# State space stage of a hybrid diffusion block: context chunks transposed first, last product of a group in the large accumulators

## The chip, the core and the metric

The kernel runs on one core of a Trainium2 chip. The metric is the device time of one execution in microseconds. TensorE (PE) does matrix products and transposes into PSUM accumulators, VectorE (DVE) and ScalarE (ACT) do elementwise work and empty the accumulators, GpSimd (POOL) does masks and small sums, and SyncE (SP) issues nearly all DMAs. Each engine takes its instructions in the order in which they were written for it.

## What is computed

One layer of a diffusion backbone over 512 latent tokens and 256 context tokens of width 1024, in fp32 throughout. The part that matters here is the bidirectional state space scan (SSD) in the token mixer, with 24 heads in 4 groups and chunks of 128 tokens. In the reference, for one direction:

```
cb = jnp.einsum('bctgn,bcsgn->bctsg', cc, bc)
y_diag = jnp.einsum('bctsg,bctsgh,bcsghp->bctghp', cb, decay, xdt)
states = jnp.einsum('bcsgn,bcsgh,bcsghp->bcghpn', bc, decay_end, xdt)
...
h_final, h_prev = lax.scan(step, h0, (jnp.moveaxis(chunk_decay, 1, 0), jnp.moveaxis(states, 1, 0)))
y_off = jnp.einsum('bctgn,bctgh,bcghpn->bctghp', cc, jnp.exp(acum), h_prev)
y = (y_diag + y_off).reshape(bn, length, nh, hp)
```

The scan over the latent tokens starts from the final states of the context's two chunks. Ahead of the scan lie one wide input projection and a short convolution with silu; behind it a gate `silu(z)`, two branch projections and a mix, and then 16 routed experts (two matrices up, one down).

## The kernel before

The program runs in stages: modulation and the first projections (to about 90 us), the SSD stage (to about 380 us), gates and the Fourier branch, the branch projections and the mix (to about 620 us), routing, and the experts.

In the SSD stage `ssd(g)` works on one group of heads, g = 0 to 3, and is woven with the *fill*: the z tiles of the group before (`zgate`, 3 tiles z00, z01, z02 for group 0) and the input projections of the next group (`xbc_tiles`, 5 tiles pj and the context's pjc). The weave alternates the two in the order of the program; the scheduler then places each engine's instructions by priority and readiness, and that order is fixed when the kernel is built. A fill tile is 24 products of 128x512 in three passes (lines 348, 349, 350), with its weights split into a high and a low part by ACT and DVE (lines 276, 277, tile whl).

A group goes through these steps:
- *Transposes* (line 542): six chunks, four of the sequence (c = 0 to 3) and two of the context (c = 4, 5). Four transposes fill one accumulator ptr, which ACT copies out (line 544) to xb, or for the context to the spare ends of Hf and Hb.
- *Context states* pcs (line 559): the context chunks weighted by DVE (xwc, line 550) and multiplied; then the *states* pst (line 566) of the sequence's chunks, chunk by chunk in both directions, each with DVE's weighting and two DVE steps for the decay (568, 571).
- *Masks* rm: for each chunk and each half of the heads a DMA brings rows of decays (line 588) into one of four slots, POOL masks them (589, 591), DVE and ACT add and exponentiate (593, 595, 597), and DVE multiplies (598, 599, 602). A mask is named by group, chunk and half: rm020 is group 0, chunk 2, first half.
- *Products* py (line 612): for each chunk 36 small products into one accumulator, half of them with each of the chunk's masks, which DVE then adds into the result (line 615). py03 is chunk 3 of group 0.

PSUM has eight accumulators of 512 columns in two pools, each handed out in turn: five `mm`, called large here (`MM`), for the projections and other wide products, and three `sd` (`SD`), for everything in `ssd`. With three, an accumulator asked for now is the one that was asked for three requests ago. A product py needs 384 of 512 columns.

Of the kernel before, what the change touches and what calls it, by code (L numbers as in the profile page):

```python
# [26 lines left out]
NCH = 4  # L27
# [34 lines left out]
def block_kernel(ctx: ExitStack, tc: tile.TileContext, a: dict, out: bass.AP):  # L62
# [18 lines left out]
    def SD(name):  # L81
        return ps.tile([P, 512], F32, name=name, tag="sd")
# [4 lines left out]
    def v(t, off, *dims):  # L87

        n = int(np.prod(dims))
        s = t[:, off:off + n]  # L90
        if len(dims) == 2:
            return s.rearrange("p (a b) -> p a b", b=dims[1])
        if len(dims) == 3:
            return s.rearrange("p (a b c) -> p a b c", b=dims[1], c=dims[2])
        return s
# [435 lines left out]
    def ssd(g):  # L531
# [2 lines left out]
        xb = S(f"xb{g}", 4)  # L534
        Hs = [S(f"Hf{g}", 5), S(f"Hb{g}", 6)]
        with tc.high_priority():
            for c in range(6):
                p = SD(f"ptr{g}_{c}")
                for i in range(4):
                    src = X[:, 512 * i + 128 * c:512 * i + 128 * c + 128] if c < 4 else \  # L540
                        B[g][:, 512 + 256 * i + 128 * (c - 4):512 + 256 * i + 128 * (c - 3)]
                    pe.transpose(p[:, 128 * i:128 * i + 128], src, ident)
                dst = xb[:, 512 * c:512 * c + 512] if c < 4 else Hs[c - 4][:, 1536:2048]
                act.copy(dst, p)
# [16 lines left out]
        for k in range(3):  # L561
            for d in range(2):
                c, n = (k, k + 1) if d == 0 else (3 - k, 2 - k)
# [39 lines left out]
                yield mk[:, 0], rb  # L603

        def products(c, parts):
            py = SD(f"py{g}{c}")
            for b, (mk, rb) in enumerate(parts):
                for hb in range(3):
                    h = 3 * b + hb
                    i, j = divmod(h, 2)  # L610
                    for k, (l, r) in enumerate(((tok(c), mk), (H(0, c), rb[:, 0]), (H(1, c), rb[:, 1]))):
                        pe.matmul(py[64 * j:64 * j + 64, 128 * i:128 * i + 128], lhsT=l[:, 64 * h:64 * h + 64], rhs=r[:, hb],  # L612
                                  start=(k == 0), stop=(k == 2))
            yv = X[:, 0:1536].rearrange("p (i t) -> p i t", i=3)[:, :, 128 * c:128 * c + 128]
            dve.tensor_add(yv, yv, v(py, 0, 3, 128))
# [4 lines left out]
        for c in range(NCH):  # L620
            nxt = list(decays(c + 1)) if c + 1 < NCH else None
            yield
            products(c, parts)
            parts = nxt
            yield
# [70 lines left out]
    for g in range(G):  # L696
        weave(PAT[g], ssd(g), chained(*([zgate(g - 1, 8 * g - 3)] if g else []), *([xbc_tiles(g + 1)] if g + 1 < G else [fourier_in()])))
# [279 lines left out]
    def softmax(c):  # L977
        def negmax_exp():
            dve.tensor_reduce(st[:, c, 0:1], aff[c], axis=AX.X, op=ALU.max, negate=True)
            act.activation(aff[c], aff[c], AF.Exp, bias=st[:, c, 0:1], accum_out=st[:, c, 1:2])  # L980
        return (lambda: dve.scalar_tensor_tensor(aff[c], lg[c][:, 128:128 + NE], rsd[:, c + 1, 1:2], lb, op0=ALU.mult,
                                                 op1=ALU.add),
                negmax_exp,
                lambda: dve.reciprocal(st[:, c, 1:2], st[:, c, 1:2]),
                lambda: dve.tensor_scalar_mul(aff[c], aff[c], st[:, c, 1:2]))
# [42 lines left out]
    f = softmax(0)  # L1028
# [474 lines left out]
```

## Time and profile before

| | |
|---|---|
| median of 3 runs | 1098.39 us (1098.13 to 1099.03) |
| the profiled execution | 1095.86 us, of which the span from first to last instruction is 1094.1 |
| PE busy | 1064.9 us, 97% of the span |
| DVE, ACT, POOL busy | 520.0, 431.5, 86.0 us |
| DMA | 293.82 MB, 269 GB/s over the span |

The busy time of PE is modelled: its matmuls overlap, so that one of 128x512 lasts 0.39 us but the next starts 0.23 us later. A wait of PE stands in square brackets behind the instruction that waited, with the instruction that released it.

### The profile page before, as it was taken

The numbers are of one execution on the slowest core, as the hardware profiler recorded it, in microseconds if no ns is written. First come the engines' busy times: TensorE is split into PE (matmuls) and PEld (weight loads), VectorE is DVE, ScalarE is ACT, GpSimd is POOL, SyncE is SP. The second block draws the span as 40 slices with busy tenths as digits, with TensorE's granted clock in tenths as the row PEclk, the third lists the DMA queues.
The fourth block names the chain that finished last, engine by engine and source line by source line (L and its number), as shares of the span: only waits on it lengthen the run. The fifth ranks groups of instructions, "written<-read, shape, count | busy, mean of one in ns | idle before, by whom it ended". The sixth has DMA issues, their size and how long they took to land.

```text
span 1094.1 us, 15349 instructions
## 1 busy us (share of the span) xinstructions
PE 1064.9 (97%) x6154; PEld 712.4 (65%) x6154; DVE 520.0 (48%) x853; ACT 431.5 (39%) x690; POOL 86.0 (8%) x119
## 2 busy tenths in 40 slices
PE   8999999999999999999999999999999999899997
PEld 5788867878878888888788634454545454444444
DVE  5776989786695666864434531212121212120206
ACT  4467786795794543242323631212021211021112
POOL 1001143021112100000100200000000000000000
PEclk9999999999999999999999999999999999999999
DMA  9613251422514358863337899999999999999996
GB/s 358 232 39 99 72 143 49 115 88 88 171 45 134 126 219 297 314 238 116 98 113 293 324 402 422 407 422 420 421 421 420 422 421 421 420 421 421 421 415 273
DMA packets 57590, 293.82 MB, mean 269 GB/s; under 512 B 6992, under 2 KB 15664, under 8 KB 30256
## 3 DMA queue, kind: packets, MB, share of 16 engines
q1 hardware_dynamic: 56800, 290.65, 68.6%
q10 hardware_dynamic: 720, 2.21, 0.6%
q8 instruction: 48, 0.79, 0.3%
q14 instruction: 22, 0.18, 0.1%
HBM read 288.52 MB, written 4.31 MB: 268 GB/s over the span
## 4 chain that ended last, share of the span: by engine, by line
PE 49%; issue 43%; DVE 3%; DMA 3%; ACT 1%; POOL 1%; POOLq 0%; SPq 0%; ACTq 0%
PE gt L350 3%; PE gt L348 3%; PE gt L349 3%; PE py L612 2%; PE pj L348 2%; PE pj L349 2%; PE pj L350 2%; DMA rm<-rowd 2%; PE sbr L350 2%; PE sbr L349 2%; PE sbr L348 2%; PE z L348 2%; PE z L350 2%; PE z L349 2%; PE pst L566 2%
## 5 line engine op out<-in xcount | busy, mean ns | idle before, releaser
L1338 DVE TENSOR_TENSOR hid<-hid,pu 128x512 f32<-128x512 f32 x16 | 11.0, 687 | 231.5 <-PE pu L1166 231.5
L1377 PE MATMUL pd<-w_ed,hidT 128*64 128x256 f32 x1024 | 115.8, 381 | 4.9 <-DMA w_ed<-in_w_ed_dram 4.7
L276 ACT CAST whl<-raw 128x1024 fp32r<-128x1024 f32 x71 | 74.4, 1050 | 114.3 <-PE gt L350 46.7
L1166 PE MATMUL pu<-w_eu,xes 128*64 128x512 f32 x512 | 115.3, 595 | 3.5 <-DMA w_eu<-in_w_eu_dram 3.5
L277 DVE TENSOR_TENSOR whl<-raw,whl 128x1024 fp32r<-128x1024 f32 x71 | 90.5, 1277 | 48.1 <-ACT whl L276 47.9
L1166 PE MATMUL pg<-w_eg,xes 128*64 128x512 f32 x512 | 111.9, 594 | 0.0
L1377 PEld LDWEIGHTS pd<-w_ed,hidT 128*64 128x64 f32 x1024 | 73.5, 137 | 43.9 <-DMA w_ed<-in_w_ed_dram 7.6
L1166 PEld LDWEIGHTS pu<-w_eu,xes 128*64 128x64 f32 x512 | 36.9, 137 | 75.8 <-issue 66.7
L1166 PEld LDWEIGHTS pg<-w_eg,xes 128*64 128x64 f32 x512 | 36.0, 137 | 69.7 <-issue 65.8
L1298 DVE SCALAR_TENSOR_TENSOR ys<-pd,afs,ys 128x512 fp32r<-128x512 f32 (+1 forms) x18 | 12.4, 691 | 111.4 <-ACT ys L1297 111.4
L1348 ACT COPY hidT<-ht 128x512 f32<-128x512 f32 x16 | 9.4, 586 | 125.5 <-PE ht L1346 125.5
L1297 ACT ACTIVATE ys<-pd,afs 128x512 fp32r<-128x512 f32 (+1 forms) x18 | 11.5, 640 | 102.7 <-PE pd L1377 61.4
L350 PE MATMUL gt<-hhi,whl 128*128 128x512 f32 x128 | 50.0, 391 | 0.0
L348 PE MATMUL gt<-hhi,whl 128*128 128x512 f32 x128 | 50.0, 391 | 0.0
L593 DVE TENSOR_TENSOR rm<-rm,misc 128x768 f32<-128x768 f32 x32 | 32.4, 1014 | 36.8 <-POOL rm L591 36.8
L349 PE MATMUL gt<-hlo,whl 128*128 128x512 f32 x128 | 49.8, 389 | 0.0
L348 PE MATMUL pj<-hhi,whl 128*128 128x512 f32 x120 | 48.6, 405 | 0.0
L350 PE MATMUL pj<-hhi,whl 128*128 128x512 f32 x120 | 48.2, 402 | 0.0
L349 PE MATMUL pj<-hlo,whl 128*128 128x512 f32 x120 | 48.0, 400 | 0.0
L671 DVE SCALAR_TENSOR_TENSOR wm<-wm,misc 128x1024 f32<-128x1024 f32 x32 | 38.1, 1221 | 13.4 <-DMA wm<-in_wmod_dram 13.4
L1320 ACT ACTIVATE hid<-pg 128x512 f32<-128x512 f32 x16 | 9.4, 597 | 82.4 <-PE pg L1166 82.4
L348 PE MATMUL z<-hhi,whl 128*128 128x512 f32 x96 | 41.3, 430 | 0.0
(436 smaller groups left out, 2301.1 us busy)
## 6 DMA issues: line engine op xcount, KB each, us to landing
w_eg<-in_w_eg_dram SPq DMA_DIRECT2D x64, 1024.0 KB, 19.8
w_eu<-in_w_eu_dram SPq DMA_DIRECT2D x64, 1024.0 KB, 19.8
w_ed<-in_w_ed_dram SPq DMA_DIRECT2D x56, 1024.0 KB, 19.8
raw<-in_w_rest_dram SPq DMA_DIRECT2D x71, 512.0 KB, 3.3
wm<-in_wmod_dram SPq DMA_DIRECT2D x16, 1024.0 KB, 6.8
rm<-rowd SPq DMA_DIRECT2D x32, 384.0 KB, 5.3
wmod<-in_wmod_dram SPq DMA_DIRECT2D x8, 1024.0 KB, 7.9
w_ed<-in_w_ed_dram SPq DMA_DIRECT2D x16, 512.0 KB, 10.9
```

The costliest lines, as they stand in the source:

```text
L276: act.copy(hi, src)
L277: dve.tensor_sub(lo, src, hi.bitcast(F32))
L348: pe.matmul(dst, lhsT=wh, rhs=hi, start=(kt == 0 and start), stop=False)
L349: pe.matmul(dst, lhsT=wh, rhs=lo, start=False, stop=False)
L350: pe.matmul(dst, lhsT=wl, rhs=hi, start=False, stop=(kt == nk - 1 and stop))
L566: pe.matmul(p[:, 0:384], lhsT=tok(c)[:, 384:512], rhs=t, start=True, stop=True)
L593: dve.tensor_tensor(mk, mk, csm[:, :, c, hs:hs + 3][:, :, :, None].to_broadcast([P, 2, 3, 128]), op=ALU.add)
L612: pe.matmul(py[64 * j:64 * j + 64, 128 * i:128 * i + 128], lhsT=l[:, 64 * h:64 * h + 64], rhs=r[:, hb], start=(k == 0), stop=(k == 2))
L671: dve.scalar_tensor_tensor(wv, wv, 1.0, crow, op0=ALU.mult, op1=ALU.mult, accum_out=mod2[:, 2 * p + s:2 * p + s + 1])
L1166: pe.matmul(pout[n][64 * e:64 * e + 64, :], lhsT=xe[kt // 4][:, kt % 4, 64 * e:64 * e + 64], rhs=w[kt // 2, e][:, o:o + 512], start=(kt == ...
L1298: dve.scalar_tensor_tensor(R(yl_), pd, afs, yh_, op0=ALU.mult, op1=ALU.subtract)
L1377: pe.matmul(pd[64 * e:64 * e + 64, o:o + 256], lhsT=hidT[kt // 4][:, kt % 4, 64 * e:64 * e + 64], rhs=wd[m, e][:, 256 * kt:256 * kt + 256] ...
```

## The change

Two lines of `ssd`. The context's chunks are transposed ahead of the sequence's, and the accumulator of the last product of each group (chunk 3) is asked for in the large pool.

```
-            for c in range(6):
+            for c in (4, 5, 0, 1, 2, 3):
                 p = SD(f"ptr{g}_{c}")
...
         def products(c, parts):
-            py = SD(f"py{g}{c}")
+            py = (MM if c == NCH - 1 else SD)(f"py{g}{c}")
```

No instruction is added or left out, but the scheduler places many of them anew. The first place is PE between groups 0 and 1, from the last products of py01 on. A row names the accumulator, then the two operands; z00 is the first fill tile of group 1's weave, ptr1_4 and ptr1_5 are the context chunks of group 1. Before:

```order
L612 MATMUL py01_1281<-rm011_1063,xb0_794 64x128
L612 MATMUL py01_1281<-rm011_1063,Hf0_795 64x128
L612 MATMUL py01_1281<-rm011_1063,Hb0_796 64x128
L348 MATMUL z00_1470<-hhi0_205,whl5_1472 128x512
L349 MATMUL z00_1470<-hlo0_207,whl5_1472 128x512
L350 MATMUL z00_1470<-hhi0_205,whl5_1472 128x512
L348 MATMUL z00_1470<-hhi0_205,whl5_1472 128x512
```

And in the changed kernel:

```order
L612 MATMUL py01_1281<-rm011_1063,xb0_794 64x128
L612 MATMUL py01_1281<-rm011_1063,Hf0_795 64x128
L612 MATMUL py01_1281<-rm011_1063,Hb0_796 64x128
L612 MATMUL py02_1329<-rm020_1220,xb0_794 64x128
L542 MATMUL ptr1_4_1372<-mats_92,B1_896 128x128 x4
L542 MATMUL ptr1_5_1378<-mats_92,B1_896 128x128 x4
L612 MATMUL py02_1329<-rm020_1220,Hf0_795 64x128
```

The 24 products of z00 and the first 3 of z01, which stood between py01 and py02, now stand behind: the first three of z00 come after the first half of py03, and when the state products pst of group 1 begin 12 z products have run where 60 had run before. On ACT the copies of these transposes stand behind the exponential (line 597) of the first mask of group 1, in the changed kernel:

```order
L597 ACTIVATE rm100_1505<-rm100_1505 128x768
L544 COPY Hf1_1370<-ptr1_4_1372 128x512
L544 COPY Hb1_1371<-ptr1_5_1378 128x512
L544 COPY xb1_1369<-ptr1_0_1384 128x512
L544 COPY xb1_1369<-ptr1_1_1390 128x512
```

Before, the same exponential stood ahead of them too, with the copies of ptr1_0 and ptr1_1 as the first. On DVE, at the masks of chunks 2 and 3 of group 0 (whl7 is the weight of z02):

```order
 L598 TENSOR_TENSOR rm021_1234<-rm021_1234 128x384
-L277 TENSOR_TENSOR whl7_1598<-raw_899,whl7_1598 128x1024
+L598 TENSOR_TENSOR rm030_1301<-rm030_1301 128x384
 L599 TENSOR_TENSOR rm021_1234<-rm021_1234,cb0_890 128x384
-L598 TENSOR_TENSOR rm030_1301<-rm030_1301 128x384
+L599 TENSOR_TENSOR rm030_1301<-rm030_1301,cb0_890 128x384
 L602 TENSOR_TENSOR rm030_1301<-rm030_1301,B0_656 128x768
```

A weight split leaves its place between the two halves of a mask and moves behind group 1's first states. Up to this place, from the first products of group 0 on, DVE's instructions are the same in number and nearly the same in order. Between groups 1 and 2, and 2 and 3, the last projection tile (pj24, pj34) stands behind the last product (py13, py23) in both kernels; now two transposes of each context chunk stand right behind the first product of py12 (py22), and the chunks of the sequence other than the first close up behind 18 products of pj24 (pj34). From the z tiles of group 3 on the order is the same in both kernels.

## Rows read from the trace of the kernel before

**Rows 1.** The page: span, and busy us of each engine (share)

```profile
span 1094.1 us, 15349 instructions
PE 1064.9 (97%) x6154; PEld 712.4 (65%) x6154; DVE 520.0 (48%) x853; ACT 431.5 (39%) x690; POOL 86.0 (8%) x119
```

**Rows 2.** Windows: us, busy us (instructions) by engine, PEclk, DMA share, GB/s

```profile
99.50:142.90 43.40, 42.80 (x255) 33.85 (x253) 41.50 (x66) 37.35 (x49) 10.50 (x15) 1.00 0.42 121
137.00:164.00 27.00, 24.69 (x159) 18.29 (x158) 24.20 (x33) 23.45 (x32) 11.10 (x13) 1.00 0.53 144
547.00:600.00 53.00, 52.94 (x234) 43.48 (x233) 20.55 (x22) 15.97 (x23) 5.16 (x4) 1.00 0.53 195
700.00:800.00 100.00, 99.66 (x606) 48.30 (x603) 15.44 (x23) 13.95 (x30) 0.00 (x0) 1.00 1.01 417
```

**Rows 3.** Waits of SP's queue on the experts' weights: us, times, longest

```profile
SPq L1158 <- PE mix L823: 16.9, 1, 16.9
```

**Rows 4.** PE timeline (start, us): its waits in the SSD stage from 100 us on

```profile
143.11 0.40 PE L612 MATMUL py<-rm,xb 128*64 128x128 f32 x2 [0.57 <-DVE rm L599]
...
156.68 0.33 PE L542 MATMUL ptr<-mats,B 128*128 128x128 f32 x1 [0.28 <-DVE A L615]
...
160.39 0.59 PE L559 MATMUL pcs<-xwc,Hf 128*128 128x384 f32 x1 [0.77 <-DVE xwc L550]
...
163.25 0.59 PE L559 MATMUL pcs<-xwc,Hf 128*128 128x384 f32 x1 [0.69 <-DVE xwc L550]
...
221.25 0.33 PE L542 MATMUL ptr<-mats,A 128*128 128x128 f32 x1 [0.75 <-DVE A L615]
...
299.42 0.33 PE L542 MATMUL ptr<-mats,A 128*128 128x128 f32 x1 [0.80 <-DVE A L615]
...
359.50 0.29 PE L612 MATMUL py<-rm,xb 128*64 128x128 f32 x1 [0.70 <-DVE rm L599]
```

**Rows 5.** PE timeline between groups 0 and 1

```profile
136.12 0.50 PE L348 MATMUL z<-hhi,whl 128*128 128x512 f32 x1
...
142.15 0.39 PE L350 MATMUL z<-hhi,whl 128*128 128x512 f32 x1
...
144.53 0.50 PE L348 MATMUL z<-hhi,whl 128*128 128x512 f32 x1
...
150.68 0.66 PE L542 MATMUL ptr<-mats,A 128*128 128x128 f32 x4
```

**Rows 6.** Windows of the z tiles' instructions alone

```profile
136.12:143.11 6.99, 6.42 (x27) 4.99 (x27) 0.00 (x0) 1.00 0.67 186
```

**Rows 7.** DVE timeline: first context weighting of group 0, masks of chunk 2

```profile
100.19 0.56 DVE L550 TENSOR_TENSOR xwc<-Hf,misc 128x384 f32<-128x384 f32 x1 [0.82 <-ACT Hf L544]
...
142.42 0.55 DVE L599 TENSOR_TENSOR rm<-rm,cb 128x384 f32<-128x384 f32 x1
...
145.89 1.21 DVE L277 TENSOR_TENSOR whl<-raw,whl 128x1024 fp32r<-128x1024 f32 x1
147.02 0.55 DVE L599 TENSOR_TENSOR rm<-rm,cb 128x384 f32<-128x384 f32 x1
```

**Rows 8.** ACT timeline: exponential of rm100, and the first copy behind it

```profile
152.06 0.84 ACT L597 ACTIVATE rm<-rm 128x768 f32<-128x768 f32 x1 [0.74 <-POOL rm L591]
154.01 0.59 ACT L544 COPY xb<-ptr 128x512 f32<-128x512 f32 x1 [1.10 <-PE py L612]
```

**Rows 9.** SP timeline: the load of mask rm100

```profile
144.75 0.36 SPq L588 DMA_DIRECT2D rm<-rowd  x1
```

**Rows 10.** Windows: the clock behind the mix

```profile
620.00:632.00 12.00, 10.09 (x77) 5.21 (x70) 9.06 (x34) 8.95 (x27) 2.39 (x5) 0.86 1.00 417
```

**Rows 11.** PE timeline: the longest wait in that stretch

```profile
627.26 0.29 PE L989 MATMUL lg<-mats,affs 128*48 128x128 f32 x1 [0.94 <-DVE affs L985]
```

## The prediction

> **What bounds the kernel now.** I read the page's busy table first: PE is busy 97% of a span of 1094.1 us [rows 1], so time is lost only where PE waits or works slower, and what another engine does counts only through a PE wait. Then the windows: around the SSD stage PE and DVE are both near full. From 99.5 to 142.9 us DVE is busy 41.50 of 43.40 us, and from 137 to 164 PE loses 2.3 of 27 us [rows 2]. Later, from 700 us on, the 16 DMA engines are at 1.01 with PE at 99.66 of 100 us [rows 2], which asks whether a shift of the SSD stage reaches the end at all. It does: the loads of that stretch go out when PE's mixing products free their buffers (the sync queue waited 16.9 us for one) [rows 3], and in between, at 547 to 600 us, PE has next to no slack (52.94 of 53 us) while DMA stands at 0.53 [rows 2]. So a microsecond that PE wins or loses in the SSD stage is a microsecond at the end, less nothing that I can point to.
>
> Last the PE timeline of the SSD stage: it shows seven waits, 4.56 us together [rows 4]. Three of them (0.28, 0.75, 0.80) are a transpose that waits for DVE's add of line 615, that is for the small accumulator that the last product of the group ahead still holds; two (0.77, 0.69) are the context state products behind their DVE weighting; two (0.57, 0.70) are a chunk product behind the mask on DVE. The change can win back 1.83 us of the first kind and 1.46 of the second, and by luck 0.57 more ahead of them: the whole prize is 0.3%.
>
> **What is removed and added.** No instruction is removed or added: the same transposes, copies, products and adds, an accumulator of the same size in another pool. What changes is the order, and the printed order tells most. I go by boundary between groups.
>
> Boundary 0 to 1, the first two excerpts. In the kernel before, product py01 ends as the z tiles begin, at 136.12 [rows 5]; PE then runs 27 matmuls of z00 and z01 (6.42 us busy in 6.99) [rows 6] and only then, at 143.11, the first product of py02, which even so waits 0.57 us [rows 4]: its mask rm020 is multiplied on DVE from 142.42 to 142.97 [rows 7]. In the changed kernel py02 stands right behind py01, and no z matmul comes before half of py03. My reading is that py03 now asks for a buffer of the large pool ahead of z00 in program order, and z00 can no longer overtake it; but whatever made it, the order is fixed and PE takes its matmuls as they stand. So the question is when rm020 is ready. On DVE it is row 192 in both orders, with the same work ahead of it, and DVE has only 1.90 us of idle time in 99.5 to 142.9 that it could have saved [rows 2]; 0.82 us of that is the start, where the first weighting waits for the copy of a context chunk [rows 7], which the change brings ahead. Against it, the bias of tile pj11 on ACT now stands behind more copies, and DVE's next instruction wants it. I take 0.5 us earlier.
> - First wait: 143.11 less 136.12 is 6.99, less 0.5 gives **6.5 us** in which PE has nothing (bounds 5.1, if DVE saves all 1.90, and 7.5, if the copies make it 0.5 later).
> - Second wait: py02's second half needs rm021, ready at 147.57 [rows 7]. The 1.21 us weight split between moves away and a 0.55 us add comes in, so 146.9. PE starts at 142.6 and has half a product (143.11 to 144.53, 1.42 us [rows 4, 5]) and two transposed context chunks (0.66 us busy for one such, a little less back to back [rows 5]), so it is there at 145.3. **1.6 us** (0.5 to 2.2).
> - Third wait: ptr1_1 needs the bank of ptr1_4, whose copy on ACT stands behind the exponential of rm100 (the excerpt on ACT). That one was at 152.06, after a mask whose load went out at 144.75 [rows 8, 9], just behind py02's first half. That half now ends 0.7 us later, so the exponential of 0.84 ends at 153.6 and a copy of 0.59 [rows 8] at 154.1; PE, from 146.9, has two half products and one more with a transposed chunk in it (3 x 1.42 and 0.66), and 8 z matmuls at 0.232 (26 of them from 136.12 to 142.15 [rows 5]), so it arrives at 153.7. **0.4 us** (0 to 1.1).
> - Removed here: 0.57, 0.28, 0.77 and 0.69, together **2.3 us**. The context transposes come long before their weighting now, and the split that stood ahead of it on DVE is gone.
> - Net at this boundary: 6.5 + 1.6 + 0.4 - 2.3 = **+6.2 us**. The 48 z matmuls that are left over cost nothing extra (PE must run them in any case), but they do not win it back either: behind this place the kernel before has only 2.25 us of waits left in the stage [rows 4].
>
> Boundaries 1 to 2 and 2 to 3. Here the tile pj24 (pj34) stood behind py13 (py23) already, so no filler is lost. The transposes of context chunks begin in front of py12's body, in banks that are long free, and the waits of 0.75 and 0.80 [rows 4] for line 615 go, since the bank of py13 is not theirs any more. In exchange ptr2_1 stands three short matmuls behind the last piece of ptr2_4 and must wait for its 0.59 us copy [rows 8]: 0.2 us each. **-1.15 us** for both (bounds -1.55 and 0). The wait of 0.70 at 359.50 hangs on the mask alone and stays.
>
> The clock. The granted clock is 1.00 through the whole stage now [rows 2]. It is 0.86 in 620 to 632 us, where PE waits 0.94 us for DVE among small products [rows 10, 11]; 12 us at 0.86 is at most 1.7 us of PE work lost. An idle stretch of 6.5 us is far longer than any that PE has in the stage. I expect 1.2 GHz for a while behind it, part of it inside the second wait: **+0.5 us** (0 to 1.7).
>
> Sum: 6.2 - 1.15 + 0.5 = **+5.5 us**. The profiled execution took 1095.86 us for its span of 1094.1, so 1101.4 by it; the median of the runs shown is 1098.39, 2.5 us above that execution, so I forecast **1103.9 us**, 0.5% slower. With all low ends: 5.1 + 0.5 - 2.3 - 1.55 = +1.75, 1100.1 us. With all high ends: 7.5 + 2.2 + 1.1 - 2.3 + 1.7 = +10.2, 1108.6 us.
>
> **The rivals.** Less than 0.2%, 2.2 us, is about what a measurement of this kernel can tell from no change.
>
> The prize alone, faster: the masks of chunk 2 are ready when py01 ends, because ACT and DVE run their share of group 0 earlier. Then the waits of transposes and weightings go (2.3 + 1.15) and nothing is added: 1098.39 - 3.45 = 1094.9 us. It decides from the point where rm020 is ready by 136.2, 6.8 us earlier than now; DVE's 1.90 us of idle time [rows 2] speak against it. For it speaks only that the profile's times are of one order of instructions, and this is another. 5%.
>
> Low ends together, about the same: ACT's copies do come early, DVE closes all its gaps, no second halt of note, and both later boundaries win their full share: +1.75, 1100.1 us. 15%.
>
> A long cold stretch: if the clock falls not once but again, since the second and third waits follow closely, two more pieces such as that of 620 to 632 cost 2 x 1.7 us less the 0.7 that the waits hide: +8.2, 1106.6 us. For it: between 136 and 154 PE would have 8.5 us of waits and then mostly small products, which is what stands around 627 too [rows 10]. Against it: no drop in the stage now, with waits up to 0.8. 25%. The Trainium skill, page "TensorE: Matmul & The Clock Gate", section "HAM oscillation — how this bites in real kernels", describes it as a habit: matmuls that wait long for data fall back to half rate at every such wait and restart cold. By that rule this rival would be the likelier, and the forecast 1106.6 rather than 1103.9; the drop near 627 agrees in kind, but no row here has a wait as long as this one.
>
> The change does little at the later boundaries (the transposes wait for ACT's copies in place of DVE's adds): that puts 1.15 us on any of these cases, and is inside their spread.
>
> **How the numbers follow.** My own sum 55%, the cold stretch 25%, the low ends 15%, the prize alone 5%. The forecast is the first, with 1101 to 1106 us as its own range. The range of 8 in 10 leaves out the prize (5%), the lowest part of the low ends and the highest of the cold stretch: 1099.8 to 1107.5 us. Slower by over 0.2% (above 1100.6 us) are the first two cases: 80%, and 0.03 of the low ends, about 82%; same 13%; faster 5%.
>
> **What would show it.** After: a PE wait of 5 to 7.5 us near 136 us, put down to DVE's line 599 and standing ahead of a py product; a second of 1 to 2 us some 3 us behind it; no wait on line 615 for a transpose near 221 and 300; z matmuls from about 150 us on instead of 136; a granted clock under 1.00 just behind the first wait. The state products of group 1 then start earlier than now (165.12) by some 5 us but with 48 z matmuls (11.1 us at 0.232) still to come. I am wrong if PE reaches py02 later than I think, if masks come several microseconds earlier, or if PE's delay is absorbed behind 600 us, where loads and PE run level.

## The result, and the profile after

The changed kernel takes 1106.95 us (median of 4 runs, 1104.88 to 1108.5) against 1098.71 us for the kernel before in the same comparison: 1.0072 times as long, 95% interval 1.0056 to 1.0088. That is 8.2 us slower, where 5.5 were forecast. The profiled execution of the changed kernel is the slowest of its four (1108.5 us) and that of before was a quick one (1095.86 us), so the two profiles lie further apart than the medians.

The page of the changed kernel, as [rows 1]:

```profile
span 1106.8 us, 15368 instructions
PE 1067.4 (96%) x6151; PEld 714.3 (65%) x6154; DVE 516.4 (47%) x853; ACT 428.9 (39%) x688; POOL 92.8 (8%) x119
```

PE's busy time is 2.5 us above that of before, while the span has grown by 12.7. Most of what was lost is PE standing still. Where, the PE timeline of the SSD stage tells (start, duration, and in brackets the idle time ahead and what ended it), as [rows 4]:

```profile
142.94 0.66 PE L612 MATMUL py<-rm,xb 128*64 128x128 f32 x2 [6.51 <-DVE rm L599]
...
155.32 0.92 PE L542 MATMUL ptr<-mats,A 128*128 128x128 f32 x6 [0.89 <-ACT Hf L544]
...
160.30 0.88 PE L559 MATMUL pcs<-xwc,Hf 128*128 128x384 f32 x2 [1.50 <-DVE xwc L550]
...
235.39 0.89 PE L559 MATMUL pcs<-xwc,Hf 128*128 128x384 f32 x2 [1.68 <-DVE xwc L550]
...
237.61 1.65 PE L559 MATMUL pcs<-xwc,Hb 128*128 128x384 f32 x2 [1.34 <-DVE xwc L550]
...
314.00 0.44 PE L542 MATMUL ptr<-mats,B 128*128 128x128 f32 x2 [0.73 <-ACT B L362]
...
319.15 0.91 PE L559 MATMUL pcs<-xwc,Hb 128*128 128x384 f32 x2 [1.21 <-DVE xwc L550]
```

Seven waits again, but now 13.9 us together instead of 4.6. The three on DVE's line 615 are gone, and so is the 0.70 at 359.50. In their place stand one of 6.51 ahead of py02, two ahead of group 1 (a transpose that waits for ACT's copy, and a context product pcs), and waits at the context products of groups 2 and 3 and at a transpose of group 3.

The windows, as [rows 2] for the first two; the other two are the stretches in which the clock was low:

```profile
99.50:142.90 43.40, 36.93 (x226) 28.95 (x224) 41.07 (x66) 37.32 (x49) 11.52 (x15) 0.98 0.44 121
137.00:164.00 27.00, 18.67 (x122) 13.76 (x123) 23.07 (x35) 18.85 (x29) 9.41 (x12) 0.87 0.39 107
141.20:148.00 6.80, 5.06 (x34) 4.43 (x35) 6.80 (x11) 5.87 (x8) 2.45 (x3) 0.50 0.22 84
236.75:243.60 6.85, 5.99 (x11) 3.79 (x12) 5.67 (x10) 2.17 (x4) 0.00 (x0) 0.50 0.23 74
```

From 137 to 164 PE is busy 18.67 of 27 us where it was 24.69. The granted clock is 0.50, that is 1.2 GHz, for 6.8 us around the end of the first wait, and for 6.85 us again from 236.75 on, at the pair of waits of 1.68 and 1.34.

The shift can be followed along PE by the starts of products that both kernels have. This table is read from the PE timelines of all runs (us; fa is the first product of the Fourier branch behind the stage; in g0_small_mask_late the first transposes of the stage already start 1.5 us later than in before, at 96.90 against 95.40):

| run | py11 | py21 | py31 | end of py33 | fa |
|---|---|---|---|---|---|
| before | 192.4 | 270.5 | 342.9 | 362.1 | 384.3 |
| after | 200.3 | 283.3 | 356.1 | 374.0 | 396.2 |
| after_again | 200.2 | 279.2 | 352.1 | 370.0 | 392.2 |
| order_only | 193.1 | 270.9 | 343.4 | 361.4 | 383.6 |
| pool_only | 200.0 | 278.1 | 352.9 | 370.8 | 393.0 |
| g0_small | 192.1 | 271.2 | 343.7 | 361.6 | 383.8 |
| g0_only | 200.0 | 278.2 | 350.7 | 369.2 | 391.4 |
| warm_wait | 200.2 | 278.6 | 352.1 | 370.0 | 392.2 |
| z00_ahead | 196.4 | 275.1 | 347.8 | 366.7 | 388.9 |
| z00_z01_ahead | 192.9 | 271.9 | 346.3 | 364.3 | 386.4 |
| after_mask_late | 199.6 | 277.4 | 349.1 | 367.1 | 389.3 |
| order_mask_late | 193.0 | 270.4 | 341.9 | 359.8 | 382.0 |
| g0_small_mask_late | 195.2 | 272.4 | 344.0 | 361.9 | 384.1 |
| z00_z01_ahead_mask_late | 192.6 | 270.3 | 341.9 | 360.0 | 382.2 |

In the first two rows: 7.9 us are lost by py11, another 4.9 between py11 and py21, 0.5 by py31, and 1.3 come back by the end of py33. The end of the kernel is later by 12.7, so the stage's loss reaches it, as the prediction argued.

### The profile page after: what moved, and what is told of

Same layout as the page of the kernel before. It is cut to its first block, busy times and chain, and to the rows that moved or that the text cites. A ratio compares the mean times of both kernels' runs of the same rounds, so it can differ in the third digit from the quotient of the medians.

```text
span 1106.8 us, 15368 instructions
## 1 busy us (share of the span) xinstructions
PE 1067.4 (96%) x6151; PEld 714.3 (65%) x6154; DVE 516.4 (47%) x853; ACT 428.9 (39%) x688; POOL 92.8 (8%) x119
## 4 chain that ended last, share of the span: by engine, by line
PE 51%; issue 42%; DMA 3%; DVE 2%; ACT 1%; POOL 1%; POOLq 0%; ACTq 0%; SPq 0%
PE py L612 3%; PE gt L350 3%; PE gt L348 3%; PE gt L349 3%; PE pj L348 2%; PE pj L349 2%; PE pj L350 2%; PE z L348 2%; PE z L349 2%; PE z L350 2%; PE sbr L350 2%; PE sbr L349 2%; PE sbr L348 2%; PE pst L566 1%; DMA rm<-rowd 1%
```

## The experiments

Two theories stood at the start. *Filler*: the whole loss begins where group 0's last product, now in the large pool, takes the z tiles' place between py01 and py02. *Order*: the context chunks ahead of the sequence's are what costs, above all at the later groups, where DVE's mask additions and the weightings of the context come into another order.

### The two halves of the change, and group 0 alone

`order_only` has the first edit alone:

```
-            py = (MM if c == NCH - 1 else SD)(f"py{g}{c}")
+            py = SD(f"py{g}{c}")
```

> Only the new order of the chunks in a group; the last product keeps its small accumulator. Filler theory (the loss starts where the z tiles of group 0 can no longer stand ahead of py02): the z matmuls stand ahead of py02 again, so no PE wait of over 0.8 us between py01 and py02 of group 0, no granted clock under 1.00 near 141 us, the state products of group 1 at 165 us as before; the time is that of before within 2 us, at best 1 us less. Order theory (the context chunks ahead of the sequence's put the weighting of the later groups behind their masks on DVE): the wait at the weighting of group 2, 1.7 and 1.3 us, and a clock of 0.5 behind it are here too, and the kernel is some 4 to 5 us slower than before.

`pool_only` has the second alone:

```
-            for c in (4, 5, 0, 1, 2, 3):
+            for c in range(6):
```

> Only the large accumulator for the last product; the chunks in their old order. Filler theory: the wait of 6 to 7 us ahead of py02 of group 0 and the half clock behind it are both here, the raw weight loads stand behind the masks as in the changed kernel, and the time is within 3 us of the changed kernel's, some 5 to 9 us above before. Order theory: the wait at group 0 is here (some 8 us at that boundary), but the 4.9 us lost between groups 1 and 2 are not, so the PE products of group 2 come 8 us late and not 13.

`g0_small` is the changed kernel with `MM if c == NCH - 1 and g else SD`, so that group 0 alone keeps its small accumulator:

> The changed kernel, but the last product of group 0 alone stays in the small accumulator. Filler theory: nothing is lost at group 0, and the loads of the later groups keep the order of before, so no wait over 1 us at group 2's weighting; the waits of 0.75 and 0.80 us on line 615 are gone too; time 0 to 2 us under before. Order theory: like order_only, 4 to 5 us above before from the boundary between groups 1 and 2.

`g0_only` is the changed kernel with `MM if c == NCH - 1 and not g else SD`:

> The changed kernel, but only the last product of group 0 is in a large accumulator; those of groups 1 to 3 stay small. Filler theory: the whole loss is here, 6 to 9 us above before, with the wait of 6 to 7 us and half clock at group 0 and the late masks of group 2. Order theory: the same at group 0, so this run does not tell the two apart there; what it tells is whether the large accumulators of groups 1 to 3 matter: if they do, this differs from the changed kernel by more than 2 us.

Measured, all against one median of before, 1097.35 us: order_only 1096.92 us (0.9990, 0.9975 to 1.0005), pool_only 1105.99 (1.0081, 1.0055 to 1.0107), g0_small 1098.12 (1.0001, 0.9987 to 1.0016), g0_only 1104.94 (1.0060, 1.0038 to 1.0081). Of these four the two with group 0's last product in the large pool are slower by 7.6 and 8.6 us, the two without it are level with before. PE timelines of pool_only and then of order_only at the place in question:

```profile
143.06 0.66 PE L612 MATMUL py<-rm,xb 128*64 128x128 f32 x2 [7.33 <-DVE rm L599]
```

```profile
142.51 0.39 PE L349 MATMUL z<-hlo,whl 128*128 128x512 f32 x1
143.15 0.40 PE L612 MATMUL py<-rm,xb 128*64 128x128 f32 x2 [0.25 <-DVE rm L599]
```

py02 starts at 143.1 in both: the mask is ready when it was. What differs is whether z matmuls fill the time ahead of it. The order theory is out as the cause of the loss.

It has a remnant, though. In order_only and g0_small the waits of 0.75 and 0.80 on line 615 are gone or down to 0.43 us (at 216.57 in g0_small; the one at group 1 is 0.39 and 0.51), and yet next to nothing was gained. The PE timeline of g0_small, where none over 1 us was expected, shows waits at the context products of groups 2 and 3 instead:

```profile
228.35 0.91 PE L559 MATMUL pcs<-xwc,Hb 128*128 128x384 f32 x2 [1.52 <-DVE xwc L550]
...
306.76 0.91 PE L559 MATMUL pcs<-xwc,Hb 128*128 128x384 f32 x2 [1.14 <-DVE xwc L550]
```

The new chunk order alone does not make these waits. With small accumulators in the later groups they are 0.69 us at most (order_only, g0_only), and pool_only, with the chunks in their old order, has them too (PE timeline):

```profile
236.11 0.91 PE L559 MATMUL pcs<-xwc,Hf 128*128 128x384 f32 x2 [1.43 <-DVE xwc L550]
...
315.31 0.91 PE L559 MATMUL pcs<-xwc,Hf 128*128 128x384 f32 x2 [2.46 <-DVE xwc L550]
```

The large accumulators of the later groups seem to have a part in them; why is open. The order theory's 4 to 5 us did not come: py21 is some 0.3 us later than before in order_only and 0.7 in g0_small.

### The changed kernel once more

> The changed kernel once more, unaltered. What is asked is whether the 4.9 us lost between groups 1 and 2 in its first profile (two waits of 1.68 and 1.34 us, then a granted clock of 0.5) belong to the kernel or to that execution: in pool_only and g0_only, with the same order of weight loads, that boundary cost nothing. If they belong to it: the time is 3 us or more above g0_only's, some 9 to 10 us above before. If not: this profile shows no half clock near 237 us, and the time is 7.5 to 8.5 us above before.

Measured: 1107.01 us (1.0085 of before, 1.0071 to 1.0099). PE timeline and the window around 237:

```profile
143.00 0.66 PE L612 MATMUL py<-rm,xb 128*64 128x128 f32 x2 [6.53 <-DVE rm L599]
...
236.40 0.91 PE L559 MATMUL pcs<-xwc,Hb 128*128 128x384 f32 x2 [1.34 <-DVE xwc L550]
```

```profile
230.00:250.00 20.00, 17.93 (x78) 12.31 (x78) 16.73 (x29) 17.92 (x26) 2.08 (x4) 1.00 0.19 64
```

The clock near 237 is 1.00, and py21 is 8.7 us late where it was 12.8 in the first profile. So 4 of the 4.9 us lost there belonged to that execution: about 1 us of them is longer waits (3.02 against 2.07 us at this boundary), and some 3 are left for the clock. The time did not fall with it, though, and was 9.25 us above before, where 7.5 to 8.5 were expected for this case. In this execution another 2.5 us went between fa and the routing (first routing product 10.4 us later than before, fa 7.9): a PE wait of 1.69 us for POOL at 447.12, 0.77 in before, and a clock of 0.89 behind it:

```profile
440.00:450.00 10.00, 8.31 (x40) 6.85 (x40) 7.05 (x12) 3.08 (x4) 2.62 (x2) 0.89 0.84 321
```

So this execution too had a second stretch of low clock, behind the stage. The loss does not hang on one, though: two executions of this run have a mean granted clock of 0.997, which leaves about 6.6 us at 1.2 GHz in some 1105 (estimated as 0.003 x 2 x 1105), no more than the first stretch alone takes, and they took 1104.85 and 1106.47 us, 7.1 and 8.7 above before. Which of the smaller waits are in every execution, two profiles can't settle.

### Keeping PE busy in the wait

`warm_wait` puts 24 matmuls on zeros into py02's accumulator ahead of its products:

```
             py = (MM if c == NCH - 1 else SD)(f"py{g}{c}")
+            if g == 0 and c == 2:
+                warm(py, 24)
```

> The changed kernel with 24 matmuls on zeros (0.218 us apart, so 5.2 us) in py02's accumulator ahead of its products, in the time in which PE waits; their result is overwritten. It keeps PE busy and leaves the filler where it is. If the half clock behind the first wait costs some 2 us, as the sum's other terms leave for it (8 us lost at that boundary, 6.2 worked out without the clock): no half clock between 141 and 148 us, the wait ahead of py02's second half (1.6 us by my sum) comes up in its place, and the products of group 1 start 1 to 2 us earlier than in the changed kernel. If the clock costs nothing, since the masks bound PE there anyway: the clock is full and py11 still starts 7.5 to 8 us late. If it is the small work and not the wait that lowers the clock, it falls all the same.

Measured: 1104.65 us (1.0062, 1.0047 to 1.0078), 2.4 us under after_again in the same comparison. But py11 starts at 200.2, as in after_again, and fa at 392.2 in both; in these two profiles the difference lies behind the stage. Windows of the kernel with zeros, and its PE wait:

```profile
136.00:146.00 10.00, 9.02 (x63) 5.02 (x60) 8.78 (x14) 9.58 (x12) 3.68 (x4) 1.00 0.46 134
146.00:151.00 5.00, 3.37 (x22) 2.88 (x22) 5.00 (x10) 1.84 (x3) 0.90 (x2) 0.66 0.34 79
```

```profile
147.63 0.66 PE L614 MATMUL py<-rm,xb 128*64 128x128 f32 x2 [2.34 <-DVE rm L599]
```

The clock stayed at 1.00 through the first wait and PE ran on at full rate, to stand 2.34 us ahead of py02's second half until 147.63. In the changed kernel PE crawls there at 1.2 GHz and starts the second half at 146.88 with no wait. The mask of that half, rm021, is the first of the two multiplied here (DVE timelines of the changed kernel and then of the kernel with zeros):

```profile
146.19 1.01 DVE L599 TENSOR_TENSOR rm<-rm,cb 128x384 f32<-128x384 f32 x2
```

```profile
146.93 1.02 DVE L599 TENSOR_TENSOR rm<-rm,cb 128x384 f32<-128x384 f32 x2
```

So in the changed kernel it is ready at 146.7, just as PE gets there: up to this mask the half clock cost next to nothing, since at full rate PE would have been there at 145.3 and waited. It is no clean removal of the clock: with the zeros the mask itself came 0.75 us later, and at the wait of 2.34 the clock fell all the same; what these took from the gain is not separated.

### The z tiles requested ahead of the last product

`z00_ahead` requests tile z00 ahead of py03 in the program, `z00_z01_ahead` (range(2)) also z01; everything of the change stays:

```
+            if g == 0 and c == NCH - 1:
+                for i in range(1):
+                    ahead[i] = MM(f"z0{i}")
+                    proj_tile(5 + i, ahead[i])
             products(c, parts)
```

> The changed kernel with the 24 z matmuls of tile z00 requested in the program ahead of group 0's last product, which keeps its large accumulator. If the loss is that the last product asks for its large accumulator ahead of z00: z00 stands between py01 and py02 again, 24 x 0.232 = 5.6 of the 6.5 us are filled, there is no half clock near 141, and the time is that of before plus 0 to 2 us; nothing else of the change is undone. If the large accumulator itself costs (banks, loads), the loss stays near 8 us.

> The same with z00 and z01 ahead, so that as much filler as before stands around py02. By the same theory no PE wait over 1 us at group 0 at all, and the waits on the small accumulator (0.28, 0.75, 0.80) gone: between before less 2 us and before. The order theory is out by now; its only remnant would be waits of 1 to 1.5 us at the weightings of groups 2 and 3, as in g0_small, which would hold the time at that of before.

Measured, with before at 1097.76: z00_ahead 1102.83 us (1.0051, 1.0034 to 1.0069), z00_z01_ahead 1098.61 (1.0008, 0.9994 to 1.0023). Nothing but the place of these tiles in the program was changed, and the fill came back. With z00 alone the expectation of 0 to 2 us was missed, since the wait moved to the next mask, that of py02's second half, where nothing is left to fill it (PE timeline of z00_ahead):

```profile
143.17 0.40 PE L613 MATMUL py<-rm,xb 128*64 128x128 f32 x2 [0.86 <-DVE rm L600]
...
148.24 0.40 PE L613 MATMUL py<-rm,xb 128*64 128x128 f32 x2 [2.41 <-ACT rm L598]
```

With both, no wait over 0.5 us stands ahead of py02, and group 0 costs 0.5 us by py11. What is left are waits of 1.34 us at the context products of groups 2 and 3, one of 1.19 at those of group 1, and, against the expectation, one of 0.97 on the add into the result ahead of a transpose of group 3 (at 296.94).

### The mask additions behind the weightings

What the context products wait for is seen on DVE. The DVE timeline of the changed kernel (first profile) ahead of group 2:

```profile
233.82 0.96 DVE L593 TENSOR_TENSOR rm<-rm,misc 128x768 f32<-128x768 f32 x1 [2.52 <-POOL rm L591]
234.69 0.55 DVE L550 TENSOR_TENSOR xwc<-Hf,misc 128x384 f32<-128x384 f32 x1
236.13 0.96 DVE L593 TENSOR_TENSOR rm<-rm,misc 128x768 f32<-128x768 f32 x1 [0.89 <-POOL rm L591]
237.00 0.55 DVE L550 TENSOR_TENSOR xwc<-Hb,misc 128x384 f32<-128x384 f32 x1
237.47 0.55 DVE L550 TENSOR_TENSOR xwc<-Hf,misc 128x384 f32<-128x384 f32 x1
```

Weightings that PE wants stand behind additions for the masks of chunk 1, which are needed only for py21, and these wait for POOL. Four kernels put the additions for chunk 1's masks behind the four weightings, in groups 1 to 3:

```
                 dve.tensor_tensor(mk, mk, csm[:, :, c, hs:hs + 3][:, :, :, None].to_broadcast([P, 2, 3, 128]), op=ALU.add)
+                if g and c == 1:
+                    tc.add_manual_dep(nc.cur_bb.bb.instructions[-1], last[g].name,
+                                      mybir.DependencyInfo(mybir.DependencyClass.NoSync, mybir.DependencyReason.DATA),
+                                      reason="order")
```

where `last[g]` is the last weighting issued ahead of them.

> The changed kernel, with one order added on DVE: in groups 1 to 3 the additions of line 593 for the two masks of chunk 1 come behind the four context weightings of line 550. In the changed kernel the fourth of these additions stands between the first and the second weighting and waits for its mask, and PE waits 1.2 to 1.7 us there at each of the groups 1, 2 and 3. Mask theory (that addition is what the context products wait for): those PE waits go at groups 2 and 3, some 1.3 us each, and the time is 2 to 3 us under the changed kernel's; group 0's loss of some 8 us stays. Rival (PE waits there because the weightings are late for another reason, the copies of lines 362 and 544 on ACT): waits only move, time within 1 us of the changed kernel's.

> order_only with the same order added on DVE. Mask theory: the 1.1 us at group 1's context products, which stand behind other work, stays; the waits of 0.4 us at groups 2 and 3 go; 0.5 to 1.5 us under order_only. Rival: as order_only.

> g0_small (the whole change but for group 0's last product) with the same order added on DVE. Mask theory: its PE waits of 1.52 and 1.14 us at the context products of groups 2 and 3 go, and it is 2 to 2.5 us under g0_small, so 1 to 2.5 us faster than before: the prize of 1.15 us that the prediction saw at the two later boundaries, and what group 1 gives. Rival: as g0_small, level with before.

> z00_z01_ahead with the same order added on DVE. Mask theory: its PE waits of 1.34 and 1.34 us at groups 2 and 3 go, and it is 2 to 2.7 us under z00_z01_ahead, 1 to 2 us faster than before. Rival: as z00_z01_ahead, 0 to 1 us slower than before.

Measured, with before at 1098.67: after_mask_late 1103.08 us (1.0037, 1.0021 to 1.0052), order_mask_late 1095.75 (0.9979, 0.9964 to 0.9994), g0_small_mask_late 1095.45 (0.9977, 0.9964 to 0.9991), z00_z01_ahead_mask_late 1095.96 (0.9977, 0.9961 to 0.9992). By its ratio to before each is below the kernel that it was made from; the intervals stand clear of each other for after_mask_late (3.8 to 5.3 us by the two comparisons, where 2 to 3 were expected) and just so for z00_z01_ahead_mask_late, touch for g0_small_mask_late, and overlap widely for order_mask_late. The last three are some 0.2% faster than the kernel before, by 2.7 to 3.2 us. In all four no context product of group 2 or 3 waits 0.2 us or more; the waits on the context's activation (line 362) stay, and so do those at the context products of group 1, 1.12 to 1.42 us. PE timeline of z00_z01_ahead_mask_late, groups 2 and 3, and the window that answers to the second of [rows 2]:

```profile
223.46 0.44 PE L544 MATMUL ptr<-mats,B 128*128 128x128 f32 x2 [0.93 <-ACT B L362]
...
301.12 0.44 PE L544 MATMUL ptr<-mats,B 128*128 128x128 f32 x2 [0.89 <-ACT B L362]
```

```profile
137.00:164.00 27.00, 25.27 (x161) 18.75 (x160) 24.10 (x35) 23.52 (x33) 7.99 (x12) 1.00 0.56 146
```

The mask theory holds for the waits at groups 2 and 3, and for the time in two of the four kernels; in the other two its gain is not clear of the noise. The three fast versions can't be told apart, so the large accumulator shows no gain of its own. What they share is the new chunk order and the mask order. How the 0.2% divides between the two is not shown: the mask order on the kernel before, where no context product of groups 2 and 3 waits [rows 4], was not tried.

## Why the prediction came out as it did

The direction and the main mechanism were right. The time lies in the range of 1099.8 to 1107.5, near its upper end, 3 us above the forecast and just outside the 1101 to 1106 that the prediction gave its own sum. The terms:

- **First wait, 6.5 us**: measured 6.51 and 6.53. The reading behind it, that py03 asks for a large buffer ahead of z00, is borne out by z00_ahead and z00_z01_ahead, where only the order of requests was changed.
- **Second wait, 1.6 us**: it is not among the waits, because PE spent the time at 1.2 GHz. The term stands all the same: PE at full rate was there at 145.3 (in warm_wait, as forecast), the mask was ready at 146.7 (146.9 forecast), and the second half started at 146.88. The 2.34 us of warm_wait are longer because its mask came later.
- **Third wait, 0.4 us**: 0.89 and, in after_again, 1.02. Mis-sized by half a microsecond; the bound was 1.1.
- **Removed, 2.3 us**: mis-sized. The 0.57 and 0.28 are gone, but not the 0.77 and 0.69 at the weighting [rows 4]: one wait of 1.50 us stands there instead (1.18 in after_again, where the profile names ACT, but PE starts 0.14 us behind the third weighting). The step that failed is "the context transposes come long before their weighting now, and the split that stood ahead of it on DVE is gone": ACT's copy of the first context chunk runs from 154.70 to 155.27, and the first weighting starts at 155.30. The transposes were early, at 143.5, but the copy was not, and the prediction's own third wait had it end at 154.1. And DVE has other mask work between the two pairs of weightings, 2.4 us in all, as its timeline in the changed kernel shows. PE's wait of 1.50 us ends with the third weighting:

```profile
156.10 0.87 DVE L550 TENSOR_TENSOR xwc<-Hb,misc 128x384 f32<-128x384 f32 x1
156.89 1.27 DVE L602 TENSOR_TENSOR rm<-rm,B 128x768 f32<-128x768 f32 x1
158.08 1.29 DVE L593 TENSOR_TENSOR rm<-rm,misc 128x768 f32<-128x768 f32 x1
159.29 0.87 DVE L550 TENSOR_TENSOR xwc<-Hf,misc 128x384 f32<-128x384 f32 x1
```

  With 6.5 for the first wait, 1.6 for the second, 0.9, 1.5 and 2.3 less, the boundary comes to 8.2; py11 was 7.9 us late.
- **Boundaries 1 to 2 and 2 to 3, -1.15 us**: wrong in sign. The waits on line 615 went, as foreseen, but the context chunks, now first, wait for ACT's activation of the context (0.41 and 1.45 us in after_again), and the context products for the weighting behind a mask addition (1.34 and 0.55). In after_again py21 and py31 lose 0.9 and 0.5 us more. I had counted one copy of 0.59 as all that could be late next, and had looked at PE's order there, not at DVE's. The 0.70 at 359.50, which I said would stay, went and gave 0.7 of the 1.3 back.
- **Clock, +0.5 us** (0 to 1.7): at the first wait its cost is inside the second wait. Once, at 237, it cost some 3 us: py21 was 12.8 us late against 8.7 without it, less the 1 us of longer waits.

Against the forecast, 1.7 us more were lost by py11 (7.9 for 6.2), and at the two later boundaries, in after_again, 1.4 us were lost where 1.15 were to be won; the end of the stage gave 1.3 back.

The number came out near the rival of the long cold stretch (+8.2, 1106.6). That is luck: its mechanism, two more cold stretches behind the second and third waits, did not come. The second stretch of the first profile stands at 237, after_again had none in the stage and was as slow, and the two executions at a mean clock of 0.997 had no room for one anywhere. The Trainium skill, page "TensorE: Matmul & The Clock Gate", section "HAM oscillation — how this bites in real kernels", says that matmuls that wait long for data restart at half rate. All five profiles with a wait of 6 us or more agree (0.50 and 0.54 in 141.2 to 148.0 in the two of the changed kernel); with waits of 1.6 to 2.5 us it went both ways, as told below.

The state products of group 1 start at 162.1, 3 us earlier than before, where I said 5, with the 48 z matmuls still to come, and z starts at 149.9 as said. The claim that the shift of the stage reaches the end held: in the first profile fa is 11.9 us later and the span 12.7 longer, in g0_only 7.1 and 9.5.

## What to carry to other kernels

A buffer's pool is also a place in the queue of requests: a tile that moves to a shared rotating pool can hold back tiles that are requested behind it, and the fill that covered a wait goes with them; look at what the order puts into the gap, and request the fill first. When a wait is taken from one engine, read on the engine that feeds the next step which instruction now stands ahead of the one that is wanted: here two mask additions were moved behind four weightings, and kernels level with before came out 0.2% below it. And compare several executions before a term is put down to the kernel, since 4 us that the stage lost in the first profile were not lost in the second.

## What was not expected of the hardware

The clock's answer to waits of middle length was not the same from one profile to the next. It fell at 2.34 us in warm_wait (0.66 over 146 to 151), at 2.46 us in pool_only (0.83 over 312 to 322) and at 1.68 and 1.34 in a row in the first profile (0.50 for 6.85 us), and not behind 2.41 us in z00_ahead:

```profile
136.00:165.00 29.00, 23.19 (x155) 16.77 (x152) 25.54 (x37) 24.46 (x34) 9.79 (x13) 1.00 0.42 120
```

A wait of 1.69 us for the same small product of the gates was followed by 0.89 in after_again, and in order_only by 1.00 over 400 to 500 us:

```profile
400.00:500.00 100.00, 98.31 (x451) 81.58 (x450) 71.93 (x110) 33.11 (x44) 2.62 (x2) 1.00 0.75 270
```

Eight of the fourteen profiles have this wait of 1.69 us. Four of them show the drop (0.91 over 436 to 456 in after_again, g0_only, after_mask_late and g0_small_mask_late), and there it takes 230.2 to 230.5 us from fa to the first routing product, against 227.4 to 229.1 in the other ten; none of the six with a wait of 0.77 shows it. What decides between the two is open. In pool_only the clock was already low while PE had nothing to do, 0.65 over 137 to 142.9 with no matmul in it, so the first products behind a long wait start slow.
